# PEER feed-forward: the last 32 tokens' experts gathered for VectorE, the dense experts on 224 columns with v's weights stationary

## The chip, the cores and the metric

The kernel runs on one core of one Trainium2 chip. The metric is the device time of one execution in microseconds. TensorE (PE) multiplies matrices, VectorE (DVE) and ScalarE (ACT) work elementwise, GpSimd (POOL) does elementwise work too, and SyncE (SP) issues most of the DMAs.

## What is computed

Two blocks of 256 tokens and model width 1024: attention with a convolutional gated MLP, then a state-space and attention mixer. What the change touches is the last feed-forward, PEER, with 16384 experts, 8 heads, and 16 picks of each head, so 128 picks of each token:

```
q = (x @ w_q).reshape(bsz, seq, PEER_HEADS, 2, PEER_KEY_DIM)
s1 = einsum('bshd,hnd->bshn', q[..., 0, :], sub_k1)
s2 = einsum('bshd,hnd->bshn', q[..., 1, :], sub_k2)
v1, i1 = lax.top_k(s1, PEER_TOPK)
v2, i2 = lax.top_k(s2, PEER_TOPK)
cand_s = v1[..., :, None] + v2[..., None, :]
cand_i = i1[..., :, None] * PEER_KEYS + i2[..., None, :]
top_s, pos = lax.top_k(cand_s, PEER_TOPK)
experts = take_along_axis(cand_i, pos, axis=-1)
gates = softmax(top_s, axis=-1)
# per token: 128 experts ec, 128 gates gc
act = gelu(einsum('ced,cd->ce', u_tab[ec], xc)) * gc
out = einsum('ce,ced->cd', act, v_tab[ec])
```

The result is added to x, and a last RMS norm gives the output.

## The kernel before

**Numbers.** Activations and weights are f32 values, each split in two parts of a type that TensorE takes at a high rate: a high part, and the rest as a low part. A product is three matmuls (hi·hi, lo·hi, hi·lo; lines 154 and 157), accumulated in PSUM. Each weight tile of 128 x 1024 is loaded by SyncE (line 81), rounded by ScalarE to `whi` (line 92), and its rest `wlo` is subtracted by VectorE or, for every `share`-th tile, by GpSimd (line 94). A helper, `Weights`, does so some tiles ahead, in the order in which tiles are taken; instructions stand on each engine in the order in which the code issues them.

**Dense experts.** The kernel does not gather. It computes u for all 16384 experts and all 256 tokens, gelu, multiplies by gates that are zero where an expert was not picked, and multiplies with all of v. This takes two stages of 128 chunks, each chunk 128 experts.

*u stage.* `u_pair` (line 1695) takes two chunks into one PSUM bank: weights of u stationary, the 256 tokens of x (`hTh`, `hTl`) moving, 24 matmuls of 256 columns to a chunk, so 48 to a pair. ScalarE applies gelu into `S` (two buffers, `S0` for chunks 0 to 63, `S1` for 64 to 127). In the first 24 pairs the routing work (top-k on VectorE) is dealt out between matmuls from a list `work`, in token halves 0 and 1, and `share` is 2 in that time, 0 afterwards.

*Gates.* In the pairs of the second half of u, and in the first chunks of v, gates are made in steps: `gate_gen` builds one-hot matrices on VectorE (lines 1667, 1671, 1675), `gate_mm` multiplies them on TensorE (line 1690, 128 x 64 in bf16, 24 matmuls on average to a step), and line 1693 multiplies `S` by the result. There are 32 steps to each half of the experts.

*v stage.* For each chunk ScalarE rounds S to `ah` (line 1775), GpSimd subtracts the rest, `al` (line 1776), and 12 matmuls follow: stationary are 128 tokens of `ah` or `al`, moving are 512 columns of v's `whi` or `wlo`; four PSUM banks hold two token halves by two column halves of the output. The order is ah·whi, ah·wlo, al·whi, four each. The two buffers of `ah` and `al` let chunk c+1 be prepared while chunk c is multiplied.

*End.* The last four chunks run bank by bank, and behind each bank come the addition to x (line 1819), the sum of squares and the gain; then a reciprocal root from Newton steps (`rsqrt`, lines 170 to 177), two scalings and two output DMAs per token half. The first half's end lies beside the second half's matmuls.

Of the kernel before, what the change touches and what calls it, by code (L numbers as in the profile page):

```python
# [135 lines left out]
class Net:  # L136
# [543 lines left out]
    def arm_norm(self, gsrc, eng=None):  # L680

        g = self.load_g(gsrc, eng=eng)
        hT = self.new_T(self.hTp, "hT")
        xn, root = {}, {}
        ms = self.xnp.tile([128, 2, 2], FT, name="ms")

        def after(t, h, c):
            if h == 0:
                xn[t] = self.scratch()
            self.nc.gpsimd.tensor_tensor(xn[t][:, c], self.x[:, t, c], g[:, c], op=OP.mult)  # L690
            self.square(self.x[:, t, c], ms[:, t, h:h + 1])
# [828 lines left out]
    def peer(self, ctx, w, hT):  # L1520
# [7 lines left out]
        S0 = sp.tile([128, 64, S], FT, name="S0")  # L1528
        scr = sp.tile([128, 16384], FT, name="S1")
# [118 lines left out]
        def route5(t):  # L1648
# [46 lines left out]
        def u_pair(c, between=None):  # L1695
            ps = self.bank()
            for x in range(2):
                wt = w.next()
                if x and between:
                    between()  # L1700
                self.mm_cols(ps[:, 256 * x:256 * x + 256], wt, hT)
            if c == 64:
                late["S1"] = sp.tile([128, 64, S], FT, name="S1")
            dst = S0[:, c:c + 2] if c < 64 else late["S1"][:, c - 64:c - 62]
            w.post(lambda: nc.scalar.activation(dst, ps.rearrange("p (a b) -> p a b", a=2), AF.Gelu_apprx_tanh))

        for t in range(2):
            w.post(nc.scalar.activation, qn[:, t], self.queries[t], AF.Copy)
# [15 lines left out]
        for t in range(2):  # L1724
# [4 lines left out]
        todo = [(x, t, n) for t in range(2) for x in range(2) for n in range(2)]  # L1729
        for i in range(9):  # L1730
            if i < 8:
                work.append((lambda i=i: pick(*todo[i]), 16))
            if i:
                work.append((lambda i=i: picked(*todo[i - 1]), 16))
            if i == 4:
                work.append((lambda: route5(0), 10))
        work.append((lambda: route5(1), 10))

        def some(budget=16):
            while work and budget >= work[0][1] // 2:  # L1740
# [30 lines left out]

        def a_split(c, dst=None):
            src = S0[:, c] if c < 64 else late["S1"][:, c - 64]
            ah, al = dst or (sp.tile([128, S], FR, name=x, bufs=2) for x in ("ah", "al"))
# [4 lines left out]
        for c in range(64, 126, 2):  # L1779
            u_pair(c, lambda: gate_steps(1, 64))  # L1780
            if c == 94:
                gate_steps(1, 64)
        A = []
        u_pair(126, lambda: A.append(a_split(0)))
        w.flush()

        def v_mm(c, A, wt, th):
            self.mm3([(acc[t][h], *(x[:, 128 * t:128 * t + 128] for x in A), *(x[:, 512 * h:512 * h + 512] for x in wt),
                       c == 0, c == 127) for t, h in th], "s")

        nxt = A.pop()
        for c in range(124):
            if c == 122:

                w.parts = Room(sp.tile([128, 64 * S], FR, name="S0"))
            A = nxt
            wt = w.next()
            nxt = a_split(c + 1)
            v_mm(c, A, wt, [(t, h) for t in range(2) for h in range(2)])
            if c % 2 == (c > 30):  # L1800
                gate_steps(1, 128)

        A = [nxt] + [a_split(125 + i, [w.parts.tile([128, S]) for _ in range(2)]) for i in range(3)]
        wts = w.take(4)
        xr = self.hTp.tile([128, 2, D], FT, name="hTh")
        gb = self.hTp.tile([128, D], FT, name="hTl")
        src = a["norm_f_g"]
        nc.sync.dma_start(out=gb, in_=bass.AP(tensor=src.tensor, offset=src.offset, ap=[[0, 128], [1, D]]))
        for t in range(2):
            nc.sync.dma_start(out=xr[:, t], in_=self.xd[t])  # L1810
        j, xg = w.parts.tile([128, 512]), self.raw.tile([128, D], FT, name="raw")
        cc = [slice(512 * h, 512 * h + 512) for h in range(2)]
        for t in range(2):
            ms = self.tiny.tile([128, 2], FT, name="ms", bufs=4)
            for h in range(2):
                for i in range(4):
                    v_mm(124 + i, A[i], wts[i], [(t, h)])
                x = xr[:, t, cc[h]]
                V.tensor_tensor(x, acc[t][h], x, op=OP.add)
                nc.scalar.activation(j, x, AF.Square, scale=D ** -0.5, accum_out=ms[:, h:h + 1])  # L1820
                G.tensor_tensor(xg[:, cc[h]], x, gb[:, cc[h]], op=OP.mult)
            r = self.rstd(ms)
            for h in range(2):
                x = xr[:, t, cc[h]]
                if h:
                    V.tensor_scalar(x, xg[:, cc[h]], r, None, op0=OP.mult)
                else:
                    nc.scalar.activation(x, xg[:, cc[h]], AF.Identity, scale=r)
                (nc.sync if h else nc.scalar).dma_start(out=self.out[0, 128 * t:128 * t + 128, cc[h]], in_=x)


    def build(self):
        tc, nc, a = self.tc, self.nc, self.a
        with ExitStack() as ctx:
            ctx.enter_context(tc.manual_schedule())
            self.setup(ctx)
            with ExitStack() as b1:
# [27 lines left out]
                        hT = self.layer(l, w, hT)  # L1865
                with ExitStack() as c2:
                    hT = self.block2(c2, w, hT)
                self.xd = self.dram.tile([2, 128, D], FT, name="xd")
                for t in range(2):
                    nc.sync.dma_start(out=self.xd[t], in_=self.x[:, t])  # L1870
# [56 lines left out]
def pack(inp):  # L1927
# [65 lines left out]
    a["vs"] = rows(f("peer_v_2")[0])  # L1993
# [39 lines left out]
```

## Time and profile before

| | us |
|---|---|
| median of 3 runs | 1715.86 (1715.3 to 1719.04) |
| profiled execution, its own time | 1715.53 |
| its span | 1713.6 |
| PE busy | 1660.6 (97%) |
| PE weight loads busy | 1468.0 (86%) |
| DVE busy | 1243.8 (73%) |
| ACT busy | 850.6 (50%) |
| POOL busy | 623.3 (36%) |

The mean granted clock of TensorE in that execution is 0.992. Shares are averages over stages with different limits, so the rows below are read by stage: u takes from about 946 to 1330 us of the span (the first pairs a little before), v the rest. A matmul's record has a modelled end, so how fast matmuls follow each other is read from their starts.

### The profile page before, as it was taken

Reading aid. Unit: us, or ns where it says so; the run is one execution under the profiler, and the core shown is the slowest. Engines: PE = TensorE matmul, PEld = TensorE weight load, DVE = VectorE, ACT = ScalarE, POOL = GpSimd, SP = SyncE. Lnnn points to the kernel's source line nnn. Section 1 sums busy time; section 2 is a strip of 40 time slices with the busy share of each in tenths; the row PEclk is TensorE's granted clock in tenths of the full one; section 3 lists DMA queues with packets and bytes.
Section 4 is the critical chain, followed back from the end, with each engine's and each line's share of the span. In section 5 each row is a group of like instructions: output and inputs, shape, how many; then the busy total and the mean of one; then the engine's idle time right before and its main releaser. Section 6 shows DMA issues by size and latency. Waiting matters only on the chain.

```text
span 1713.6 us, 29782 instructions
## 1 busy us (share of the span) xinstructions
PE 1660.6 (97%) x11558; PEld 1468.0 (86%) x11558; DVE 1243.8 (73%) x2248; ACT 850.6 (50%) x1298; POOL 623.3 (36%) x534
## 2 busy tenths in 40 slices
PE   7999999999999999989989999999999999999998
PEld 6788898887889898768879999999999888888886
DVE  6775897767767776696743999677877889864445
ACT  6555554655555465543444445534344444445544
POOL 2213539332048834590020554000000343345555
PEclk9999999999999999989999999999999999999999
DMA  7444455654345567723444455654545555556564
GB/s 247 140 142 137 148 176 179 213 185 134 124 159 174 172 199 252 274 87 101 159 165 164 164 177 193 194 170 157 168 156 168 161 173 163 171 183 196 191 193 158
DMA packets 84717, 294.08 MB, mean 172 GB/s; under 512 B 10800, under 2 KB 14928, under 8 KB 83680
## 3 DMA queue, kind: packets, MB, share of 16 engines
q1 hardware_dynamic: 83184, 286.19, 51.3%
q0 software_dynamic: 960, 5.47, 0.9%
q8 instruction: 90, 1.47, 0.3%
q14 instruction: 51, 0.42, 0.1%
q10 hardware_dynamic: 432, 0.53, 0.1%
HBM read 284.42 MB, written 7.34 MB: 170 GB/s over the span
## 4 chain that ended last, share of the span: by engine, by line
PE 76%; DVE 12%; ACT 3%; POOL 3%; issue 3%; DMA 2%; ACTq 0%; DVEq 0%; POOLq 0%
PE acc L157 27%; PE side L157 17%; PE acc L154 14%; PE side L154 9%; DVE wlo L94 4%; PE side L1690 3%; DVE cv L776 1%; ACT whi L92 1%; DMA raw<-in_ws 1%; PE side L396 1%; POOL BB L967 1%; PE side L373 1%; DMA Kst<-dKst 1%; PE side L372 1%; DVE S L1508 1%
## 5 line engine op out<-in xcount | busy, mean ns | idle before, releaser
L94 DVE TENSOR_TENSOR wlo<-raw,whi 128x1024 fp32r<-128x1024 f32 x472 | 622.1, 1326 | 308.0 <-ACT whi L92 307.2
L92 ACT ACTIVATE whi<-raw 128x1024 fp32r<-128x1024 f32 x511 | 532.5, 1056 | 473.6 <-PE acc L157 233.0
L1776 POOL TENSOR_TENSOR al<-S,ah 128x256 fp32r<-128x256 f32 x125 | 171.4, 1371 | 443.3 <-ACT ah L1775 423.0
L154 PE MATMUL side<-hTh,whi 128*128 128x256 f32 x1664 | 235.5, 284 | 5.9 <-ACT whi L92 5.8
L157 PE MATMUL side<-hTh,wlo 128*128 128x256 f32 x1664 | 232.8, 282 | 1.0 <-DVE wlo L94 1.0
L157 PE MATMUL side<-hTl,whi 128*128 128x256 f32 x1664 | 233.0, 283 | 0.0
L154 PEld LDWEIGHTS side<-hTh,whi 128*128 128x128 f32 x1664 | 215.1, 191 | 10.3 <-ACT whi L92 7.2
L157 PEld LDWEIGHTS side<-hTh,wlo 128*128 128x128 f32 x1664 | 213.5, 191 | 1.4 <-DVE wlo L94 1.2
L157 PEld LDWEIGHTS side<-hTl,whi 128*128 128x128 f32 x1664 | 214.0, 191 | 0.0
L94 POOL TENSOR_TENSOR wlo<-raw,whi 128x1024 fp32r<-128x1024 f32 x39 | 98.9, 2539 | 129.0 <-ACT whi L92 126.5
L154 PE MATMUL acc<-whi,ah 128*128 128x512 f32 x496 | 134.2, 392 | 0.0
L157 PE MATMUL acc<-wlo,ah 128*128 128x512 f32 x496 | 132.7, 389 | 0.0
L157 PE MATMUL acc<-whi,al 128*128 128x512 f32 x496 | 132.7, 389 | 0.0
L154 PE MATMUL acc<-whi,hTh 128*128 128x512 f32 x384 | 123.9, 417 | 1.6 <-ACT whi L92 1.6
L157 PE MATMUL acc<-wlo,hTh 128*128 128x512 f32 x384 | 117.4, 400 | 0.7 <-DVE wlo L94 0.5
L157 PE MATMUL acc<-whi,hTl 128*128 128x512 f32 x384 | 117.2, 399 | 0.3 <-DVE hTl L220 0.3
L157 PEld LDWEIGHTS acc<-whi,al 128*128 128x128 f32 x496 | 93.1, 188 | 19.7
L157 PEld LDWEIGHTS acc<-wlo,ah 128*128 128x128 f32 x496 | 93.1, 188 | 19.6
L784 POOL TENSOR_TENSOR th<-th,cv 128x256 f32<-128x256 f32 x44 | 58.3, 1327 | 138.2 <-DVE th L783 109.4
L154 PEld LDWEIGHTS acc<-whi,ah 128*128 128x128 f32 x496 | 91.9, 188 | 18.1
L776 DVE SCALAR_TENSOR_TENSOR cv<-side,cw,cv 128x254 f32<-128x254 f32 (+1 forms) x176 | 72.6, 474 | 29.1 <-ACT cv L773 29.1
L157 PEld LDWEIGHTS acc<-wlo,hTh 128*128 128x128 f32 x384 | 72.9, 190 | 19.5 <-DVE wlo L94 1.8
(459 smaller groups left out, 2434.0 us busy)
## 6 DMA issues: line engine op xcount, KB each, us to landing
raw<-in_ws SPq DMA_DIRECT2D x259, 512.0 KB, 4.2
raw<-in_us SPq DMA_DIRECT2D x128, 512.0 KB, 3.8
raw<-in_vs SPq DMA_DIRECT2D x128, 512.0 KB, 4.2
dBst<-Bst SPq DMA_DIRECT2D x1, 2048.0 KB, 7.3
dCT<-CT SPq DMA_DIRECT2D x2, 1024.0 KB, 8.1
tg<-dBst POOLq DMA_DIRECT2D x1, 2048.0 KB, 11.4
gb<-in_g_ffn SPq DMA_DIRECT2D x2, 512.0 KB, 5.2
s5bc<-in_s5bc SPq DMA_DIRECT2D x2, 512.0 KB, 5.4
```

The lines of the kernel that those rows point to most:

```text
L92: self.nc.scalar.activation(hi, t, AF.Copy)
L94: eng.tensor_tensor(lo, t, hi.bitcast(FT), op=OP.subtract)
L154: mm(ps, sh, mh, start=first, stop=False)
L157: mm(ps, sl if side == "s" else sh, ml if side == "m" else mh, start=False, stop=last and side == late)
L372: nc.tensor.matmul(ps[:, 0:128], u["q"][:, 0:128], u["k"][:, 0:128], start=True, stop=True)
L373: nc.tensor.matmul(ps[:, 128:384], u["q"][:, 128:256], u["k"][:, 0:256], start=True, stop=True)
L396: nc.tensor.transpose(ps[:, 128 * i:128 * i + 128], u["p"][:, 128 * i:128 * i + 128], self.ident)
L776: nc.vector.scalar_tensor_tensor(o[which][:, n:], p[which][:, :S - n], cw[which][:, 2 - n:3 - n], o[which][:, n:], op0=OP.mult, op1=OP.add)
L784: nc.gpsimd.tensor_tensor(th, th, o[1], op=OP.mult)
L967: G.tensor_tensor(o[i][p, :, g2], t[0][p], t[1][p], op=op)
L1690: nc.tensor.matmul(o, e2[:, n], e1[:, n, x], start=x == 0, stop=x == 2)
L1776: G.tensor_tensor(al, src, ah.bitcast(FT), op=OP.subtract)
```

## The change

Tokens 224 to 255 leave the dense computation. All dense tiles have N = 224 token columns: u's moving operand, S, and gates (28 steps per half instead of 32). In v the operands change places: `whi` or `wlo` slices of 128 output columns are stationary and the 224 tokens of `ah` or `al` move, so v takes 24 matmuls to a chunk, the output is transposed, and the end turns it back with 16 TensorE transposes.

The 32 tokens' 4096 picks stand on 128 partitions by 32 (four groups of partitions, each with 32 of a token's picks). `pairs` makes their expert numbers `eid`. `dot_step(n)`, one for each u pair from the 29th on, has GpSimd issue an indirect DMA of 128 rows of u (a new input `un`, three buffers `rows`), and VectorE multiply the rows fetched two steps earlier with the tokens' x (`xs`) and sum along the row. `sum_step(n)`, one for each second v chunk from 52 on, does the same with rows of v, scaled and accumulated; two f32 matmuls with a 0/1 matrix `picks` add the four groups, and the result is added to x. `xs` comes from 32 normalized rows spilled to DRAM and read four times. Routing runs on token half 1 first. GpSimd takes every sixth weight split in the second half of u. The final loads of x and the gain move from SyncE behind v to ScalarE's queue at chunk 8 of v. The end handles output columns in three pieces, and takes one root for both halves.

```
+        N, GR = S - NS, 128 // NS
+        for g in range(GR):
+            nc.sync.dma_start(out=xs[NS * g:NS * g + NS], in_=self.hd)
+        hTd = tuple(x[:, :, 0:N] for x in hT)
...
+        def fetch(table, n):
+            if n < NS:
+                r = sp.tile([128, D], FT, name="rows", bufs=3)
+                G.indirect_dma_start(out=r, out_offset=None, in_=table,
+                                     in_offset=bass.IndirectOffsetOnAxis(ap=eid[:, n:n + 1], axis=0))
+                fetched.append(r)
+        def dot_step(n):
+            fetch(a["un"], n)
+            if 2 <= n < NS + 2:
+                r = fetched.popleft()
+                V.scalar_tensor_tensor(r, r, 1.0, xs, op0=OP.mult, op1=OP.mult, accum_out=dots[:, n - 2:n - 1])
...
+        def sum_step(n):
+            fetch(vn, n)
+            if 2 <= n < NS + 2:
+                r, y, m = fetched.popleft(), late["sum"], dots[:, n - 2:n - 1]
...
+                    V.scalar_tensor_tensor(y, r, m, y, op0=OP.mult, op1=OP.add)
+            if n == NS + 1:
+                for h in range(2):
+                    ps = self.bank()
+                    nc.tensor.matmul(ps, late["picks"], late["sum"][:, 512 * h:512 * h + 512], start=True, stop=True)
...
-                self.mm_cols(ps[:, 256 * x:256 * x + 256], wt, hT)
+                self.mm_cols(ps[:, 256 * x:256 * x + N], wt, hTd)
...
-        for t in range(2):
+        for t in (1, 0):
             for i in range(0, 16, 2):
                 work += zip(route1(t, i), (12, 8))
...
+        for c in range(64, 128, 2):
+            w.share = 6
...
+                u_pair(c, lambda: gate_steps(1, NQ))
+            dot_step((c - U0) // 2)
...
-            self.mm3([(acc[t][h], *(x[:, 128 * t:128 * t + 128] for x in A), *(x[:, 512 * h:512 * h + 512] for x in wt),
-                       c == 0, c == 127) for t, h in th], "s")
+            self.mm3([(acc[k // 2][:, 256 * (k % 2):256 * (k % 2) + N], *(x[:, 128 * k:128 * k + 128] for x in wt), *A[i],
+                       c == 0 and k % 2 == 0, last and k % 2 == 1 and i == len(A) - 1) for k in ks for i, wt in enumerate(wts)], "s")
...
+            if c >= V0 and c % 2 == 0:
+                sum_step((c - V0) // 2)
...
+                nc.tensor.transpose(late["turn"][t][tok[t], 128 * (k - k0):128 * (k - k0) + 128],
+                                    oT[k // 4][:, k % 4, 128 * t:128 * t + tok[t].stop], self.ident)
...
+        r = self.rsqrt(v, 2)
```

TensorE, one chunk of v. Before (stationary and moving operand behind the arrow in the program's order: moving first):

```order
L154 MATMUL acc<-whi,ah 128x512 x4
L157 MATMUL acc<-wlo,ah 128x512 x4
L157 MATMUL acc<-whi,al 128x512 x4
```

and now:

```order
L156 MATMUL acc<-ah,whi 128x224 x8
L159 MATMUL acc<-al,whi 128x224 x8
L159 MATMUL acc<-ah,wlo 128x224 x8
```

`al` is now asked for behind eight matmuls, where it was behind eight of 512 columns; the whole chunk has 24 instead of 12.

GpSimd, the v stage: `al` is the low part of S, `rows` the gathered rows. Before:

```order
L1776 TENSOR_TENSOR al<-S_9259,ah 128x256 x64
L1776 TENSOR_TENSOR al<-S_12131,ah 128x256 x61
L1776 TENSOR_TENSOR S_18723<-S_12131,S_18723 128x256 x3
```

and now, a piece from the middle:

```order
L1837 TENSOR_TENSOR al<-S_9261,ah 128x224 x2
L1686 DMA rows<-in_vs,eid 128x1024
L1837 TENSOR_TENSOR al<-S_9261,ah 128x224 x2
L1686 DMA rows<-in_vs,eid 128x1024
L1837 TENSOR_TENSOR al<-S_9261,ah 128x224 x2
L1686 DMA rows<-in_vs,eid 128x1024
L1837 TENSOR_TENSOR al<-S_12161,ah 128x224 x2
```

An indirect DMA stands in front of every second `al`.

VectorE, the second half of u: `wlo` is a weight split, `e` and `eq` are the one-hot matrices, `S` times `side` the gates, `rows` times `xs` a dot. Before:

```order
L94 TENSOR_TENSOR wlo<-raw,whi 128x1024
L1693 TENSOR_TENSOR S_9259<-S_9259,side 128x64x8 x2
L94 TENSOR_TENSOR wlo<-raw,whi 128x1024
L1667 TENSOR_TENSOR e_14554<-itb,ixT 128x1024
L1671 TENSOR_TENSOR eq<-itb,ixT 128x512
L1675 TENSOR_TENSOR e_14558<-eq,gT 128x1536
L94 TENSOR_TENSOR wlo<-raw,whi 128x1024 x2
```

and now:

```order
L96 TENSOR_TENSOR wlo<-raw,whi 128x1024
L1750 TENSOR_TENSOR S_9261<-S_9261,side 128x64x8 x2
L1724 TENSOR_TENSOR e_13757<-itb,ixT 128x1024
L1728 TENSOR_TENSOR eq<-itb,ixT 128x512
L1732 TENSOR_TENSOR e_13761<-eq,gT 128x1536
L1695 SCALAR_TENSOR_TENSOR rows,dots<-rows,xs 128x1024
L96 TENSOR_TENSOR wlo<-raw,whi 128x1024 x2
```

Each pair has one instruction more, `rows` times `xs`, and some splits are missing, since GpSimd has them.

## Rows read from the trace of the kernel before

**Rows 1.** Windows: us, busy by engine (instructions), clock, DMA share, GB/s.
```profile
core 0: us, PE busy (x) PEld busy (x) DVE busy (x) ACT busy (x) POOL busy (x), PEclk, DMA share, GB/s
946.00:1084.20 138.20, 137.22 (x1144) 137.02 (x1143) 134.84 (x416) 69.11 (x82) 67.48 (x25) 1.00 0.56 182
1084.20:1130.30 46.10, 46.10 (x422) 46.06 (x421) 28.11 (x30) 21.13 (x27) 0.00 (x0) 1.00 0.56 181
1140.00:1326.00 186.00, 186.00 (x2087) 185.36 (x2086) 142.42 (x176) 73.97 (x86) 0.00 (x0) 1.00 0.51 162
...
1510.00:1690.00 180.00, 180.00 (x837) 149.09 (x836) 86.53 (x74) 91.06 (x133) 96.46 (x66) 1.00 0.60 190
690.00:710.00 20.00, 18.72 (x90) 14.60 (x90) 12.83 (x33) 10.82 (x16) 7.08 (x2) 1.00 0.98 392
```

**Rows 2.** Timeline, PE around a gate step in u: start us, us, line, shapes, xcount.
```profile
1166.04 1.57 PE L1690 MATMUL side<-e,e 128*128 128x64 bf16 x48
...
1168.48 1.12 PE L157 MATMUL side<-hTl,whi 128*128 128x256 f32 x8
...
1169.44 1.12 PE L157 MATMUL side<-hTh,wlo 128*128 128x256 f32 x8
```

**Rows 3.** Timeline, one chunk of v, PE, ACT and POOL.
```profile
1600.55 1.47 POOL L1776 TENSOR_TENSOR al<-S,ah 128x256 fp32r<-128x256 f32 x1 [1.25 <-ACT ah L1775]
...
1601.63 1.07 PE L154 MATMUL acc<-whi,ah 128*128 128x512 f32 x4
...
1602.80 0.40 ACT L1775 ACTIVATE ah<-S 128x256 fp32r<-128x256 f32 x1
...
1603.44 1.07 PE L157 MATMUL acc<-whi,al 128*128 128x512 f32 x4
...
1604.35 1.07 PE L154 MATMUL acc<-whi,ah 128*128 128x512 f32 x4
```

**Rows 4.** Timeline, PE runs of other shapes, from three places.
```profile
693.56 1.08 PE L154 MATMUL acc<-hTh,whi 128*40 128x256 f32 x8
...
694.47 1.07 PE L157 MATMUL acc<-hTl,whi 128*40 128x256 f32 x8
...
712.41 1.89 PE L1246 MATMUL side<-u,tg 128*128 128x64 f32 x16
...
907.38 1.06 PE L1595 MATMUL side<-S 128*128 128x128 f32 x8
```

**Rows 5.** DVE groups by form, 1140 to 1326 us; the last row 946 to 1084.
```profile
L94 DVE TENSOR_TENSOR wlo<-raw,whi 128x1024 fp32r<-128x1024 f32 x57 | 69.7, 1223 | 43.4 <-ACT whi L92 43.4
L1675 DVE TENSOR_TENSOR e<-eq,gT 128x1536 bf16<-128x1536 bf16 x29 | 27.8, 958 | 1.0
L1667 DVE TENSOR_TENSOR e<-itb,ixT 128x1024 bf16<-128x1024 bf16 x30 | 20.5, 684 | 0.3 <-PE side L1690 0.3
L1693 DVE TENSOR_TENSOR S<-S,side 128x512 f32<-128x512 f32 x30 | 19.2, 680 | 0.0
L1671 DVE TENSOR_TENSOR eq<-itb,ixT 128x512 bf16<-128x512 bf16 x30 | 12.5, 418 | 0.0
...
L94 DVE TENSOR_TENSOR wlo<-raw,whi 128x1024 fp32r<-128x1024 f32 x24 | 36.5, 1523 | 1.1 <-ACT whi L92 0.8
```

**Rows 6.** Timeline, POOL: a DMA issue, and a weight split.
```profile
891.90 0.60 POOL L1532 DMA_DIRECT2D it<-in_iota  x1 [9.41 <-ACT S L106]
...
946.98 2.40 POOL L94 TENSOR_TENSOR wlo<-raw,whi 128x1024 fp32r<-128x1024 f32 x1 [3.35 <-ACT whi L92]
```

**Rows 7.** Timeline, the tail.
```profile
1705.34 0.69 DVE L1819 TENSOR_TENSOR hTh<-acc,hTh 128x512 f32<-128x512 f32 x1 [0.57 <-PE acc L157]
...
1707.69 0.21 DVE L177 TENSOR_SCALAR rs_y<-rs_t,rs_y 128x1 f32<-128x1 f32 x1
...
1709.12 0.72 ACT L1828 ACTIVATE hTh<-raw,rs_y 128x512 f32<-128x512 f32 x1 [2.27 <-DVE rs_y L177]
```

**Rows 8.** The page's DMA issues: count, KB each, us to landing.
```profile
raw<-in_us SPq DMA_DIRECT2D x128, 512.0 KB, 3.8
```

More of the change, by code (lines that the diff above doesn't have):

```diff
@@ L35 @@
 NEG = -1e30
+NS = 32
 EPS = 1e-6
@@ L1660, in route5, with pairs @@
                     g = grest
+        def pairs():
+            s = slice(128 - NS, 128)
+            for g in range(GR):
+                p, c = slice(NS * g, NS * g + NS), slice(NS * g, NS * g + NS)
+                V.scalar_tensor_tensor(eidf[p], sel[s, 0, 1, c], 128.0, sel[s, 1, 1, c], op0=OP.mult, op1=OP.add)
+                V.tensor_copy(gs[p], sel[s, 2, 1, c])
+            V.tensor_copy(eid, eidf)
+        fetched = deque()
+        def fetch(table, n):
[10 more added lines that the diff above has]
+            if n == NS + 1:
+                nc.scalar.activation(dots, dots, AF.Gelu_apprx_tanh)
+                V.tensor_tensor(dots, dots, gs, op=OP.mult)
+                late["sum"] = sp.tile([128, D], FT, name="xs")
+        def sum_step(n):
+            fetch(vn, n)
+            if 2 <= n < NS + 2:
+                r, y, m = fetched.popleft(), late["sum"], dots[:, n - 2:n - 1]
+                if n == 2:
+                    V.tensor_scalar(y, r, m, None, op0=OP.mult)
+                else:
+                    V.scalar_tensor_tensor(y, r, m, y, op0=OP.mult, op1=OP.add)
+            if n == NS + 1:
+                for h in range(2):
+                    ps = self.bank()
+                    nc.tensor.matmul(ps, late["picks"], late["sum"][:, 512 * h:512 * h + 512], start=True, stop=True)
+                    x = late["xr"][128 - NS:128, 1, 512 * h:512 * h + 512]
+                    w.post(V.tensor_tensor, x, ps[128 - NS:128], x, op=OP.add)
+        vn = a["vs"].rearrange("a b c -> (a b) c")
         def gate_gen(hf, q):
@@ L1723, in peer @@
             work.append((lambda t=t: route2(t), 2))
-        for t in range(2):
+        for t in (1, 0):
             for h in range(0, 8, 2):
@@ L1728, in peer @@
             work += zip(gates(t), (3, 6))
-        todo = [(x, t, n) for t in range(2) for x in range(2) for n in range(2)]
+        todo = [(x, t, n) for t in (1, 0) for x in range(2) for n in range(2)]
         for i in range(9):
@@ L1735, in peer @@
             if i == 4:
-                work.append((lambda: route5(0), 10))
-        work.append((lambda: route5(1), 10))
+                work.append((lambda: route5(1), 10))
+                work.append((pairs, 8))
+        work.append((lambda: route5(0), 10))
         def some(budget=16):
@@ L1777, in a_split, with v_mm @@
             return ah, al
[L1779 to L1787, printed above, removed]
-            self.mm3([(acc[t][h], *(x[:, 128 * t:128 * t + 128] for x in A), *(x[:, 512 * h:512 * h + 512] for x in wt),
-                       c == 0, c == 127) for t, h in th], "s")
+        for c in range(64, 128, 2):
+            w.share = 6
+            if c == 126:
+                w.share = 0
+                A = []
+                u_pair(c, lambda: (gate_steps(1, NQ), A.append(a_split(0))))
+                w.flush()
+            else:
+                u_pair(c, lambda: gate_steps(1, NQ))
+            dot_step((c - U0) // 2)
+        acc = acc[0] + acc[1]
+        def v_mm(c, A, wts, ks, last=False):
+            self.mm3([(acc[k // 2][:, 256 * (k % 2):256 * (k % 2) + N], *(x[:, 128 * k:128 * k + 128] for x in wt), *A[i],
+                       c == 0 and k % 2 == 0, last and k % 2 == 1 and i == len(A) - 1) for k in ks for i, wt in enumerate(wts)], "s")
         nxt = A.pop()
@@ L1798, in peer @@
             nxt = a_split(c + 1)
-            v_mm(c, A, wt, [(t, h) for t in range(2) for h in range(2)])
+            v_mm(c, [A], [wt], range(8))
             if c % 2 == (c > 30):
-                gate_steps(1, 128)
-        A = [nxt] + [a_split(125 + i, [w.parts.tile([128, S]) for _ in range(2)]) for i in range(3)]
-        wts = w.take(4)
[L1805 to L1808, printed above, removed]
@@ L1809, in peer @@
-        for t in range(2):
[L1810 to L1814, printed above, removed]
-            for h in range(2):
[L1816 to L1824, printed above, removed]
+                gate_steps(1, 2 * NQ)
@@ new lines, in peer @@
+            if c == 8:
+                xr = late["xr"] = self.hTp.tile([128, 2, D], FT, name="hTh")
+                gb = self.hTp.tile([128, D], FT, name="hTl")
+                src = a["norm_f_g"]
+                nc.scalar.dma_start(out=gb, in_=bass.AP(tensor=src.tensor, offset=src.offset, ap=[[0, 128], [1, D]]))
+                for t in range(2):
+                    nc.scalar.dma_start(out=xr[:, t], in_=self.xd[t])
+                late["picks"] = sp.tile([128, 128], FT, name="it")
+                nc.scalar.dma_start(out=late["picks"], in_=a["sums"])
@@ new lines, in peer @@
+            if c >= V0 and c % 2 == 0:
+                sum_step((c - V0) // 2)
+        A = [nxt] + [a_split(125 + i, [w.parts.tile([128, N]) for _ in range(2)]) for i in range(3)]
+        wts = w.take(4)
+        oT = [sp.tile([128, D], FT, name="rows", bufs=3)[:, 0:4 * N].rearrange("p (k n) -> p k n", k=4) for _ in range(2)]
+        j = w.parts.tile([128, 512])
+        xg = [self.raw.tile([128, D], FT, name="raw") for _ in range(2)]
+        ms = self.tiny.tile([128, 2, 3], FT, name="ms3")
@@ new lines, in peer, with turn @@
+        pieces = [(0, 4), (4, 6), (6, 8)]
+        tok = [slice(0, 128), slice(0, N - 128)]
+        def turn(k):
+            i = max(i for i in range(3) if pieces[i][0] <= k)
+            k0, k1 = pieces[i]
+            if k == k0:
+                late["turn"] = [self.bank() for _ in range(2)]
+            for t in range(2):
+                nc.tensor.transpose(late["turn"][t][tok[t], 128 * (k - k0):128 * (k - k0) + 128],
+                                    oT[k // 4][:, k % 4, 128 * t:128 * t + tok[t].stop], self.ident)
+            if k < k1 - 1:
+                return
+            c = slice(128 * k0, 128 * k1)
+            for t in range(2):
+                x = xr[:, t, c]
+                V.tensor_tensor(x[tok[t]], late["turn"][t][tok[t], 0:128 * (k1 - k0)], x[tok[t]], op=OP.add)
+                nc.scalar.activation(j[:, 0:128 * (k1 - k0)], x, AF.Square, scale=D ** -0.5, accum_out=ms[:, t, i:i + 1])
+                G.tensor_tensor(xg[t][:, c], x, gb[:, c], op=OP.mult)
@@ new lines, in peer @@
+        for b in range(4):
+            for k in (2 * b, 2 * b + 1):
+                v_mm(124, A, wts, [k], True)
+            for i in range(2):
+                src, dst = acc[b][:, 256 * i:256 * i + N], oT[b // 2][:, 2 * (b % 2) + i]
+                if i:
+                    nc.scalar.activation(dst, src, AF.Copy)
+                else:
+                    V.tensor_copy(dst, src)
+            for k in (2 * b - 2, 2 * b - 1) if b else ():
+                turn(k)
+        turn(6)
+        turn(7)
```

44 lines of the change are left out of this document (29 added, 15 removed).

## The prediction, made before the changed kernel had run

> **What bounds the kernel now.** I read the windows view of the expert stages first [rows 1]. Between 946 and 1690 us TensorE is busy for 137.22 of 138.20, 46.10 of 46.10, 186.00 of 186.00 and 180.00 of 180.00 us in the four stretches that matter, at a granted clock of 1.00 (its 2.4 GHz level): every gap between matmuls counts, and work on another engine only where that engine becomes later than TensorE. One is close: VectorE, 134.84 of 138.20 us in the first stretch. Then the timeline of one gate step among the u matmuls [rows 2], one chunk of v [rows 3], places where TensorE runs other shapes [rows 4], VectorE's groups [rows 5], GpSimd's instructions [rows 6] and the tail [rows 7].
>
> **Spacing now.** Eight 256-column matmuls start .96 us before the next eight [rows 2]: 120 ns each, so a u pair of 48 takes 5.76 us. A v chunk is 12 of 512 columns in 2.72 us (1601.63 to 1604.35) [rows 3], 226.7 ns each. Forty-eight gate matmuls and the eight behind them take 2.44 us [rows 2]; less .96 the gates cost 1.48, so .74 per step (24 matmuls).
>
> **The new spacing X, the term that decides.** All dense matmuls get 224 columns; no row has that. From 256 to 512 columns a column costs (226.7 - 120)/256 = .417 ns; down to 224 this gives 120 - 13.3 = 106.7. That is one end. The other is 120, no gain at all. Between them lies what a weight load allows. An f32 matmul is recorded as two passes, each with its own load of 128 weight columns; eight passes over 128 columns are busy for 1.06 us [rows 4], and with the last one's modelled duration (I estimate .275, from 1.12 less seven times .120 in rows 2) taken off, seven intervals of .112 remain. Sixteen passes over 64 columns take 1.89 [rows 4], (1.89 - .275)/15 = .108: half the columns and nearly the same spacing, so it isn't the columns that set it, and the load is what they share. With only 40 weight columns in the load, 256 columns take (694.47 - 693.56)/8 = 114 ns [rows 4] against 120. I take X = 112, since the load stands in every new matmul and these rows lie nearest in columns from below; both ends are kept.
>
> **u stage (24 matmuls per chunk, as before).** First 24 pairs: TensorE alone needs 24 x 48 x .112 = 129.0, VectorE 134.84 [rows 1]; VectorE's routing is the same work in another order, so 138.2 becomes 134.8: -3.4. Next 8 pairs: VectorE 28.1 of 46.1, so 43.0: -3.1. Second half before: 32 x 5.76 + 32 x .74 = 208.0. After: 32 x 48 x .112 = 172.0, and 28 steps (56 groups of four tokens for 64) at .74 = 20.7, together 192.7. VectorE there: of 64 weight splits every sixth goes to GpSimd, 53.3 x 1.223 = 65.2; 28 x (.958 + .684 + .680 + .418 = 2.74) = 76.7 [rows 5]; 30 dot instructions of 128x1024 with two f32 inputs. No row has such an instruction; the plain subtraction of that size is 1.22 [rows 5], I take 1.30: 39.0. Sum 180.9. GpSimd's 10.7 splits also hold VectorE up: in the first stretch 24 VectorE splits average 1523 instead of 1223 ns beside 25 instructions of GpSimd, nearly all of them splits [rows 1, 5]; 24 x .30 = 7.2, spread over some 24 splits of GpSimd's .30 for each; the other end is their whole 2.40 alone [rows 6]. I take .30, the same instruction beside VectorE: 3.2. VectorE's 184.1 stays under TensorE; for holdups between two engines so nearly equal I add 1.0, what TensorE lost in the first stretch (138.20 - 137.22). So 193.7: -14.3. u together -20.8.
>
> **v stage.** 128 x 12 x .2267 = 348.2 becomes 128 x 24 x .112 = 344.1: -4.1. Turning the operands round doubles the matmuls, so v gains nearly nothing though 32 columns are gone. Four gate steps fewer: -3.0. Twelve transposes between the last matmuls x .112: +1.3; two f32 matmuls of 512 columns for the gathered sum, four passes x .227 x 2 = +1.8. VectorE gets 32 sums x 1.30 = 42, most after the gates, where it has 180 - 86.5 us free [rows 1]. Together -4.0.
>
> **What is queued behind the gathers.** Each gather is issued by GpSimd between `al` subtractions, one per two v chunks. `al` of a chunk ends at 1602.02 (1600.55 + 1.47), .39 after its chunk began (1601.63), and is wanted 1.81 after [rows 3]. In the new order whi·al stands second, after 8 x .112 = .90. If a gather starts as an `al` ends, its issue time G and the next `al` (1.47 x 224/256 = 1.29) must be done by 2.69 + .90: .39 + G + 1.29 <= 3.59, so G <= 1.9. Rows have a direct GpSimd issue of .60 [rows 6]; an indirect one isn't shown, and I bound it by .60 and by GpSimd's longest nearby instruction, 2.40 [rows 6], whose excess of .5 in each of 32 gathers costs 16. I take under 1.9: 0, covered by TensorE's own matmuls. The rows themselves are wanted two steps later (2 x 5.4 us), where 0.5 MB loads land in 3.8 [rows 8]. Traffic grows by .5 MB per 6 us, 87 GB/s on 181; the trace has moved 392 at a share of .98 [rows 1], so weights still come in time. In u the splits on GpSimd stand behind gathers too, but are asked for two tiles ahead.
>
> **Start and tail.** The spill of 32 rows and the four reloads stand on SyncE ahead of the whole peer stage, the first dot behind 30 of its u pairs: 0, up to 3 if weight loads behind them are late. The final row and gain loads move to ScalarE's queue at chunk 8: 0. The tail grows: after the last accumulation both halves must be copied out (.4, as `ah` [rows 3]), transposed and added (.5), and one Newton root for two columns has six more small VectorE instructions, .21 each [rows 7], less .3 from a shorter last addition; a second ScalarE scaling of .72 [rows 7] follows the first. .4 + .5 + 1.3 - .3 + .72 = +2.6; bounds 0 and 5.
>
> **Sum.** -20.8 - 4.0 + 2.6 = -22.2 against the profiled execution's own 1715.5 (span 1713.6), .3 under the median shown: 1693.
>
> **Rivals.**
> (a) X stays 120: something paces a matmul whatever its columns up to 256. For: 114 and 120 at equal columns. Against: 112 at 128 and 64. u: only the 4 gate steps, -3.0; v: 3072 x .120 = 368.6, +20.4 - 3.0 + 3.1; tail +2.6. Sum +20: 1736.
> (b) VectorE and GpSimd exclude each other wholly in u's second half. VectorE then has 180.9 + 10.7 x 2.40 = 206.6, and with 34 gather issues of .60, 227.0. Instead of -14.3 this gives -1.4 to +19: 1706 to 1727. For: GpSimd's splits there beside a full VectorE were never run; against: the .30.
> (c) The slower side, by one mechanism: the gather's issue in v, pinned behind VectorE, delays `al`. If it has to sit out one split (1.23) and one sum (1.30), G = .60 + 2.53 = 3.1, 1.2 over the 1.9, and 32 x 1.2 = 39 gives 1732. From G = 1.9 + 22/32 = 2.6 it is slower than before. For: `al` itself takes 1.47 beside a VectorE split for a quarter of its width [rows 3]. Against: while VectorE is free there half the time, a short issue need not wait.
> The Trainium skill, "SBUF — State Buffer", section "SBUF: two separate sides", speaks for (c): a GpSimd-issued DMA of some 620 ns alone took some 3100 beside a VectorE copy, since descriptors wait for a shared port. No run here shows it yet; by its 3.1 the time would be that of (c).
> (d) X is column bound, 106.7. u: -3.4, -5.1, and the second half is held by VectorE at 185.1, -22.9; v 3072 x .1067 = 327.8, -20.4 + .1; tail +2.6: 1666, or 1677 where each GpSimd split costs VectorE 1.36. For: the slope from 256 to 512. Against: 112 at fewer columns.
> The Trainium skill, "TensorE: Matmul & The Clock Gate", section "Back-to-back issue gap", would go further: columns/2.4 + 2.5, 95.8 ns at 224. The trace disagrees at 256, 120 against its 109.
> (e) The split-precision type has no full rate under 256 columns. No such matmul has fewer in this kernel, so no row excludes it. Like f32 (two passes of .112 per 128 columns, [rows 4]) a matmul would take .224 x 224/128 = .39: u 3072 x (.39 - .12) = 829 more, v 3072 x .39 - 348 = 850 more, about 3390.
>
> **How the numbers follow.** Forecast .48, own range 1686 to 1706; (a) .12; (b) .13; (c) .13; (d) .09; (e) .05. A measurement of this kernel tells .2%, 3.4 us, from no change. Faster: .48 + .09 + .05 of (b) + .02 of (c) = .64. Same: .05 of (b), .02 of (c) = .07. Slower: .12 + .03 + .09 + .05 = .29. The range goes from 1672, inside (d), to 1737, with (a); outside lie (e), half of (d) and the far part of (c).
>
> **What would show it.** In the new trace: eight 224-column u matmuls starting .90 us apart (107 ns: .85, 120: .96); a v chunk of 2.69 without gates; the u stage's second half near 194 us with TensorE's idle time put down to nothing, not to `wlo`; `al` never the releaser of TensorE; gather issues under 1.9 us. I am wrong if TensorE waits for `wlo` or `al` over 5 us in all, or if its spacing is outside 109 to 115.

## The result, and the profile after

The changed kernel takes 1691.88 us (median of 4, 1691.01 to 1696.48) where the kernel before takes 1716.49 beside it: ratio .986, 95% interval .9838 to .9882, 24.6 us faster. The forecast was 1693, in a range of 1672 to 1737. The profiled execution of the changed kernel is the longest of the four, 1696.48 with a span of 1694.3; where that matters, it is said.

The windows view of the kernel before, cut at the same places of the program as the next one: u's first 24 pairs, its next 8, its other 32, and v from the start of its first matmul to the end of its last (columns as in [rows 1]):

```profile
937.90:1077.76 139.86, 138.88 (x1158) 138.68 (x1157) 136.50 (x444) 71.30 (x84) 69.89 (x26) 1.00 0.54 177
1077.76:1124.16 46.40, 46.40 (x389) 46.40 (x388) 29.48 (x31) 22.55 (x29) 0.00 (x0) 1.00 0.58 184
1124.16:1332.16 208.00, 208.00 (x2306) 207.31 (x2305) 156.79 (x192) 83.28 (x97) 1.47 (x1) 1.00 0.52 163
1332.16:1705.30 373.14, 373.14 (x2306) 309.09 (x2304) 255.32 (x261) 175.38 (x260) 177.05 (x130) 1.00 0.56 178
```

The changed kernel, the same four:

```profile
943.30:1078.50 135.20, 131.74 (x1159) 130.97 (x1158) 131.88 (x452) 69.84 (x85) 70.09 (x26) 0.99 0.56 180
1078.50:1121.68 43.18, 43.18 (x389) 43.18 (x388) 32.75 (x35) 21.88 (x29) 6.18 (x5) 1.00 0.74 247
1121.68:1314.10 192.42, 192.42 (x2210) 192.04 (x2209) 183.73 (x229) 81.63 (x98) 71.26 (x39) 1.00 0.75 254
1314.10:1683.10 369.00, 367.69 (x3760) 365.67 (x3759) 279.35 (x271) 172.77 (x261) 189.26 (x161) 1.00 0.68 226
```

| stretch (all in us) | forecast | profiles |
|---|---|---|
| before u (937.90 to 943.30) | 0 (0 to 3) | +5.4 |
| u, first 24 pairs | -3.4 | -4.7 |
| u, next 8 pairs | -3.1 | -3.2 |
| u, other 32 pairs | -14.3 | -15.6 |
| v | -4.0 | -4.1 |
| tail (8.30 to 11.20) | +2.6 | +2.9 |
| outside the span (1.93 to 2.18) | 0 | +.25 |
| sum | -22.2 | -19.05 = 1696.48 - 1715.53 |

The first line belongs mostly to this execution: in the profiles of the ten kernels below, all with the same start, u begins at 937.9 to 941.0 us, middle 939.5, so +1.6 rather than +5.4; in this one TensorE's granted clock was .83 between 770 and 780 us, where the kernel before had 1.00. The first 24 pairs also lost 1.7 us in this execution: at a wait of 2.06 us for `wlo` the clock fell to its 1.2 GHz level (granted .64 on average from 1000.5 to 1003.9 us), and sixteen matmuls took 3.48 us (1001.52 to 1005.00) instead of 1.79. With +1.6, and without this 1.7, the sum is -24.5, near the medians' difference. TensorE's timeline there:

```profile
1001.52 2.05 PE L159 MATMUL side<-hTh,wlo 128*128 128x224 f32 x8 [2.06 <-DVE wlo L96]
1003.37 1.79 PE L156 MATMUL side<-hTh,whi 128*128 128x224 f32 x8
1005.00 1.05 PE L159 MATMUL side<-hTl,whi 128*128 128x224 f32 x8
```

TensorE among the u matmuls and in one chunk of v of the changed kernel, with GpSimd and VectorE there (timeline; start us, us):

```profile
986.27 1.05 PE L156 MATMUL side<-hTh,whi 128*128 128x224 f32 x8
987.17 1.06 PE L159 MATMUL side<-hTl,whi 128*128 128x224 f32 x8
...
1559.41 1.06 ACT L94 ACTIVATE whi<-raw 128x1024 fp32r<-128x1024 f32 x1 [1.33 <-PE acc L159]
1560.11 1.06 PE L156 MATMUL acc<-ah,whi 128*128 128x224 f32 x8
1560.38 0.38 ACT L1836 ACTIVATE ah<-S 128x224 fp32r<-128x224 f32 x1
1560.84 1.42 POOL L1837 TENSOR_TENSOR al<-S,ah 128x224 fp32r<-128x224 f32 x1 [1.19 <-ACT ah L1836]
1561.65 1.70 DVE L1709 SCALAR_TENSOR_TENSOR xs<-rows,dots,xs 128x1024 f32<-128x1024 f32 x1
1562.42 1.76 POOL L1686 DMA_INDIRECT rows<-in_vs,eid  x1 [0.16 <-issue]
1562.79 1.06 PE L156 MATMUL acc<-ah,whi 128*128 128x224 f32 x8
1564.19 0.81 POOL L1837 TENSOR_TENSOR al<-S,ah 128x224 fp32r<-128x224 f32 x1
...
1565.47 1.06 PE L156 MATMUL acc<-ah,whi 128*128 128x224 f32 x8
```

Eight matmuls take .90 us in u, so 112 ns each, and a chunk of v takes 2.68 (1562.79 to 1565.47) where it took 2.72 [rows 3]. The gather occupies GpSimd for 1.76 us and the `al` behind it ends at 1565.00, .47 before its chunk begins; in the kernel before it ended .39 after [rows 3]. No wait of TensorE for `wlo` or `al` is listed for u's second half, and in v only .9 us for tiles of the last chunks and .5 at the sum's two matmuls.

### The profile page after: what moved, and what is told of

The parts are those of the page before. It is cut to its first block, busy times and chain, and to the rows that moved or that the text cites. A ratio compares the mean times of both kernels' runs of the same rounds, so it can differ in the third digit from the quotient of the medians.

```text
span 1694.3 us, 32761 instructions
## 1 busy us (share of the span) xinstructions
PE 1631.9 (96%) x12922; PEld 1500.4 (89%) x12922; DVE 1294.9 (76%) x2315; ACT 847.1 (50%) x1307; POOL 715.8 (42%) x610
## 4 chain that ended last, share of the span: by engine, by line
PE 71%; DVE 14%; POOL 5%; ACT 5%; issue 3%; DMA 2%; ACTq 0%; POOLq 0%; SPq 0%; DVEq 0%
PE acc L159 27%; PE side L159 14%; PE acc L156 14%; PE side L156 7%; DVE wlo L96 4%; PE side L1747 2%; ACT whi L94 2%; DVE cv L778 2%; POOL th L786 1%; DMA raw<-in_ws 1%; PE side L398 1%; DMA Kst<-dKst 1%; PE side L375 1%; POOL bt L965 1%; PE side L374 1%
## 5 line engine op out<-in xcount | busy, mean ns | idle before, releaser
L156 PE MATMUL side<-hTh,whi 128*128 128x224 f32 (+1 forms) x1664 | 228.5, 280 | 6.1 <-ACT whi L94 6.1
L159 PE MATMUL side<-hTh,wlo 128*128 128x224 f32 (+1 forms) x1664 | 226.0, 278 | 2.7 <-DVE wlo L96 2.3
L159 PE MATMUL side<-hTl,whi 128*128 128x224 f32 (+1 forms) x1664 | 224.3, 277 | 0.0
L1837 POOL TENSOR_TENSOR al<-S,ah 128x224 fp32r<-128x224 f32 x125 | 131.7, 1054 | 173.5 <-ACT ah L1836 172.9
L156 PE MATMUL acc<-ah,whi 128*128 128x224 f32 x992 | 132.5, 276 | 0.0
L159 PE MATMUL acc<-ah,wlo 128*128 128x224 f32 x992 | 131.0, 274 | 0.0
L159 PE MATMUL acc<-al,whi 128*128 128x224 f32 x992 | 131.0, 274 | 0.0
L156 PEld LDWEIGHTS acc<-ah,whi 128*128 128x128 f32 x992 | 120.8, 192 | 0.5 <-issue 0.5
L159 PEld LDWEIGHTS acc<-al,whi 128*128 128x128 f32 x992 | 120.8, 192 | 0.0
L159 PEld LDWEIGHTS acc<-ah,wlo 128*128 128x128 f32 x992 | 120.7, 192 | 0.0
L159 PEld LDWEIGHTS acc<-wlo,hTh 128*128 128x128 f32 x384 | 73.2, 191 | 19.2 <-DVE wlo L96 1.3
```

The costliest lines, as they stand in the source:

```text
L156: mm(ps, sh, mh, start=first, stop=False)
L159: mm(ps, sl if side == "s" else sh, ml if side == "m" else mh, start=False, stop=last and side == late)
```

## The experiments

Edits are against the changed kernel.

**v turned back.** The end is that of the kernel before, on 128 and 96 rows.

```
-            self.mm3([(acc[k // 2][:, 256 * (k % 2):256 * (k % 2) + N], *(x[:, 128 * k:128 * k + 128] for x in wt), *A[i],
...
+            self.mm3([(acc[t][h][tok[t]], *(x[:, 128 * t:128 * t + tok[t].stop] for x in A), *(x[:, 512 * h:512 * h + 512] for x in wt),
...
```

> The changed kernel with v turned back: 128 or 96 of the 224 tokens stationary, 512 columns of v moving, 12 matmuls to a chunk, the end of before without transposes; all else as changed. Theory (a weight load paces 224-column matmuls at about 112 ns, so v gained only .04 us per chunk by turning): chunks of 2.72 instead of 2.68 us, 124 x .04 = +5.0, no 16 transposes -1.8, the shorter end -1.2: +2 us against the changed kernel, 1694. Rival (turning v is what makes the 32 tokens less pay in v): 96 stationary columns cost as much as 128, so all of 32/256 of v's 344 us comes back, +40, 1732.

1700.88 us (median of 5, ratio .9911, .9898 to .9925): 9 slower than the changed kernel, clear of its interval, so more than the +2 of my theory and far from +40. TensorE's timeline in that kernel:

```profile
1599.96 1.11 PE L159 MATMUL acc<-wlo,ah 128*128 128x512 f32 x4
...
1602.76 1.09 PE L159 MATMUL acc<-wlo,ah 128*128 128x512 f32 x4
```

A chunk takes 2.80 here, 2.78 on average, so a 512-column matmul 232 ns and not the 226.7 of [rows 3]: 124 chunks x .10 = +12, less a cheaper end. Two more runs looked for the reason.

```
+            self.mm3([(acc[t][h], *(x[:, 96 * t:96 * t + 128] for x in A), ...
```

> The kernel with v turned back (the first run here), with 128 stationary tokens in both halves, the second half taking tokens 96 to 223; the output of the second half is not placed rightly. v's 512-column matmuls followed at 231 to 232 ns in that run against 226.7 in the kernel before. Theory (96 stationary tokens are the reason): 226.7 again, chunks 2.72. Rival 1 (the reason lies elsewhere, in the narrower tiles or the traffic): 231 stays, chunks 2.78.

2.78 to 2.79 again (1703.11): not the 96 stationary tokens.

```
-            ah, al = dst or (sp.tile([128, N], FR, name=x, bufs=2) for x in ("ah", "al"))
+            ah, al = dst or (sp.tile([128, S], FR, name=x, bufs=2)[:, 0:N] for x in ("ah", "al"))
```

> The kernel with v turned back (the first run), with ah and al tiles of 256 columns, of which 224 are used, so that they lie in memory as in the kernel before. Theory (the place of the stationary tiles makes 512-column matmuls follow at 231 instead of 226.7): 226.7 and chunks of 2.72. Rival (not the tiles, but what else goes on, gathers and traffic): 231 and 2.78.

2.78 again (1700.37): not the tiles' width. The chunks ahead of the first gather have it as well, so not the gathers. Nor is 232 peculiar to this build: the 512-column matmuls of the layers ahead of PEER follow at 232 to 235 ns (medians) in the kernel before as well, and v of the kernel before, at 227, is the exception. Why it is stays open. Turning v was worth 9 us in this kernel all the same, most of it by that unexplained difference.

**Without the gathers.** `dot_step`, `sum_step` and `pairs` are not called.

> The changed kernel without the gathers, the dots, the sums and their two matmuls; the PEER output of the last 32 tokens is left out. Theory (gathers lie wholly beside TensorE): only the 2.4 us of the two matmuls and their wait go: 1689 to 1690. Rival (gathers cost through the port, the DMA traffic or GpSimd's queue): 10 us or more faster, below 1682.

1688.35 (median of 5, ratio .9841, .9828 to .9855), 3.5 faster than the changed kernel by the medians, with intervals that overlap, and far from the rival's 10. Its windows for u's second half and v, same cuts:

```profile
1115.29:1307.65 192.36, 192.36 (x2210) 192.04 (x2209) 152.47 (x166) 81.24 (x97) 25.89 (x11) 1.00 0.54 176
1307.65:1674.15 366.50, 365.69 (x3756) 364.82 (x3755) 229.68 (x237) 172.50 (x261) 152.43 (x129) 1.00 0.56 182
```

u's second half is 192.36 against 192.42, though VectorE has 31 us and the DMAs 78 GB/s less: its gathers and 31 dots cost nothing there. v is 2.5 shorter (366.50 against 369.00): the two f32 matmuls for the sum (their chunks take 4.73 and 3.07 instead of 2.68, 2.44 together).

**More issue time on GpSimd in v.** One or two small gathers, read by nobody, behind each gather (one of 128 columns, or two of 64; the second is shown):

```
+            for _ in range(2 if n < NS else 0):
+                e = sp.tile([128, 64], FT, name="rows2", bufs=4)
+                G.indirect_dma_start(out=e, out_offset=None, in_=a["iota"].rearrange("p (a b) -> (p a) b", b=64),
+                                     in_offset=bass.IndirectOffsetOnAxis(ap=eid2[:, n:n + 1], axis=0))
```

> The changed kernel with a second indirect gather (128 rows of a 128-wide table, read by nobody) behind each gather in the v stage, so that GpSimd is held about 3.4 us instead of 1.76 in front of every second al. In the changed kernel's trace al ends .46 us before its chunk starts and is wanted .90 after, 1.36 to spare. Theory (al late beyond that margin holds TensorE): 1.7 - 1.36 = .3 us late, or up to .95 where al then falls beside a weight split and takes 1.42 instead of .81: 32 x .3 to .95 = +10 to +30, with al as TensorE's releaser. Rival (the issue time of a gather doesn't matter since the queue catches up): within 2 us of the changed kernel.

With one more: 1697.32 (median of 4, ratio .9888, .9873 to .9903), 5.4 slower than the changed kernel, between the two theories; the two intervals just overlap (.9882 and .9873), so the profile says more. A small gather took only .95 us plus .30 in front of it, so GpSimd was held 3.0; `al` ended up to .88 us after its chunk's start, just ahead of the .90, and TensorE lost .04 to .14 in some chunks, 1.7 in v. Another .7 lies in u's next 8 pairs (43.93 instead of 43.20), just behind the five VectorE copies that make the small gathers' row numbers. The rest of the 5.4 isn't placed.

> The changed kernel with two extra small gathers behind each gather of v, each held GpSimd some 1.25 us (.95 and .30 of issue) in the run with one. With one, al ended up to .87 us after its chunk's start and is wanted at .90. Theory: 1.25 us later again, so TensorE waits 1.2 us for al in each of 32 double chunks, +35 to +40 against the changed kernel, about 1730, slower than the kernel before: the slower rival of the prediction, with its point where the issue takes 3.0 instead of 1.9 us. Rival (al overtakes elsewhere and nothing waits): within 5 us of 1695.

With two (a single run): 1749.04, slower than the kernel before; v took 423.20 us, 54 more than in the changed kernel. Its timeline, then its window of v and its list of TensorE's waits there (total us, times, longest):

```profile
1600.79 0.96 POOL L1691 DMA_INDIRECT rows<-in_vs,eid  x1 [0.16 <-issue]
...
1601.36 1.23 DVE L96 TENSOR_TENSOR wlo<-raw,whi 128x1024 fp32r<-128x1024 f32 x1 [1.25 <-ACT whi L94]
...
1602.06 1.35 POOL L1711 DMA_INDIRECT rows<-in_iota,eid  x1 [0.31 <-issue]
...
1603.71 0.94 POOL L1711 DMA_INDIRECT rows<-in_iota,eid  x1 [0.30 <-issue]
...
1604.67 3.27 POOL L1846 TENSOR_TENSOR al<-S,ah 128x224 fp32r<-128x224 f32 x2
...
1606.38 1.15 PE L159 MATMUL acc<-al,whi 128*128 128x224 f32 x8 [1.68 <-POOL al L1846]
```

```profile
1312.00:1735.20 423.20, 385.26 (x3760) 378.86 (x3759) 290.47 (x271) 173.19 (x261) 259.87 (x225) 0.97 0.63 202
PE acc L159 <- POOL al L1846: 36.6, 24, 1.7
```

This is the slower rival (c), as a mechanism: an `al` behind too long an issue holds TensorE, 1.5 us on average and at most 1.7. These waits, 24 listed for 32 gathers, are 36.6 of the 54 us; each is longer than the 1.2 expected, since a late `al` falls beside VectorE's split and sum and takes 1.64 instead of .81. The other 17.6 us are TensorE busy longer (385.26 against 367.69) with the same number of matmuls: the granted clock over v is .97 where the changed kernel has 1.00, and behind one of the waits, between 1486.5 and 1490 us, it is .57. The clock makes some 13 of the 17.6, an estimate from .03 x 423; the expectation had only the waits. The point where TensorE begins to wait is 3.0 us, not 1.9.

**A ladder of widths.** 22 of the 24 matmuls of a u chunk on other widths in the first half of u, and v's chunks 60 to 123 on fewer columns; the columns left out are missing from the sums.

> The changed kernel with other moving widths: u chunks by eights with 256, 256, ... stepwise 256 (24 chunks... pairs 1 to 6), 240 (6 pairs), 208 (6), 192 (6), 160 (4), 128 (4) columns in 22 of 24 matmuls, then 224 in the rest; in v 224 to chunk 59, then 192, 160 and 128 columns for 20, 20 and 24 chunks. Columns left out are left out of the sums. Theory (a floor by the weight load, and 13 ns over the columns above it): median spacing 120 ns at 256, 113.3 at 240, 112 at 224 and the same 112 at 208, 192, 160 and 128. Rival 1 (spacing follows the columns): 100 at 208, 93 at 192, 80 at 160, 67 at 128. Rival 2 (the split type loses its rate at some width): several times 112 from there on.

TensorE's timeline at 256, 240 and 128 columns in u, and at 128 in v:

```profile
947.02 1.12 PE L1764 MATMUL side<-hTh,whi 128*128 128x256 f32 x8
947.98 1.12 PE L1766 MATMUL side<-hTl,whi 128*128 128x256 f32 x8
...
978.32 1.06 PE L1764 MATMUL side<-hTh,whi 128*128 128x240 f32 x8
979.21 1.06 PE L1766 MATMUL side<-hTl,whi 128*128 128x240 f32 x8
...
1109.17 1.06 PE L1766 MATMUL side<-hTl,whi 128*128 128x128 f32 x8
1110.06 1.10 PE L1769 MATMUL side<-hTh,wlo 128*128 128x128 f32 x8
...
1635.05 1.06 PE L156 MATMUL acc<-ah,whi 128*128 128x128 f32 x8
1635.94 1.06 PE L159 MATMUL acc<-al,whi 128*128 128x128 f32 x8
```

The starts lie .96 us apart at 256 columns and .89 to .90 at 240 and at 128; medians of single spacings are 120 at 256, 112 at 240, and 111 to 112 at 224, 208, 192, 160 and 128. Nothing under 240 columns gets faster, nothing gets slower: 1693.63 (a single run) for the whole kernel, like the changed one although a good part of its columns is gone. Rival (d) and rival (e) of the prediction are both out.

**No sixths on GpSimd.** `w.share = 0` in u's second half.

> The changed kernel with all weight splits of u's second half on VectorE (none of the sixths on GpSimd). Theory (splits cost VectorE about 1.22 each and little when GpSimd has them; TensorE is held only where VectorE goes past it): VectorE's 183.7 us of 192.4 become 183.7 + 10 x 1.22 less the collisions with GpSimd's ten, at most 22 us less, so 174 to 196 against TensorE's 192.4: 0 to +4 us, 1692 to 1696. Rival (VectorE and GpSimd exclude each other wholly, so the sixths cost more than they relieve): faster by 2 or more, below 1690.

1690.63 (median of 5, ratio .985, .9836 to .9865), the changed kernel's time. Its window of u's second half, then VectorE's groups there, the changed kernel's first, this one's behind:

```profile
1116.12:1308.50 192.38, 192.38 (x2211) 192.06 (x2210) 179.30 (x239) 81.40 (x98) 47.69 (x29) 1.00 0.72 255
```

```profile
L96 DVE TENSOR_TENSOR wlo<-raw,whi 128x1024 fp32r<-128x1024 f32 x54 | 65.2, 1220 | 6.0 <-ACT whi L94 6.0
L1695 DVE SCALAR_TENSOR_TENSOR rows<-rows,xs 128x1024 f32<-128x1024 f32 x31 | 37.8, 1219 | 0.0
L1724 DVE TENSOR_TENSOR e<-itb,ixT 128x1024 bf16<-128x1024 bf16 x28 | 34.6, 1237 | 0.4 <-PE side L1747 0.4
```

```profile
L96 DVE TENSOR_TENSOR wlo<-raw,whi 128x1024 fp32r<-128x1024 f32 x64 | 77.2, 1223 | 10.8 <-ACT whi L94 10.8
...
L1724 DVE TENSOR_TENSOR e<-itb,ixT 128x1024 bf16<-128x1024 bf16 x28 | 19.2, 684 | 0.0
```

VectorE has ten splits more and is busy 4.4 us less (179.30 against 183.73). The ten on GpSimd took 12.0 us off its splits and put 15.4 on the one-hot compares: nine of the 28 were held, by 1.7 each (the tenth split met a small product of the dots, 2.0 instead of .2). How, the changed kernel's timeline shows:

```profile
1156.09 2.40 POOL L96 TENSOR_TENSOR wlo<-raw,whi 128x1024 fp32r<-128x1024 f32 x1 [5.13 <-ACT whi L94]
1156.61 2.44 DVE L1724 TENSOR_TENSOR e<-itb,ixT 128x1024 bf16<-128x1024 bf16 x1
```

A compare of .68 that starts inside a GpSimd split ends .56 us behind it (1159.05 against 1158.49), and so do the other eight, wherever in the split they start: it stood until GpSimd was done. The gate products, which read one of their inputs from PSUM, keep their .68 inside the same splits. The time is the same because TensorE bounds this half in both.

**More splits on GpSimd in the first 24 pairs**, `i % 5 in (0, 2, 4)` in place of every second.

> The changed kernel with 3 of 5 instead of 1 of 2 weight splits on GpSimd in u's first 24 pairs. In its trace TensorE needs 24 x 5.36 = 128.7 there and took 135.2 (133.6 to 133.9 in the profiles of the runs before this one). Theory (VectorE's routing and splits bound that stretch): some 5 splits less on VectorE, 5 x 1.22 less what GpSimd's holds it up: -2 to -5 us, 1687 to 1690. Rival (the waits there come from single long instructions in the routing and from GpSimd's own lateness, 2.4 us a split against 2.68 per tile): within 2 us, or slower.

1693.48 (median of 5, ratio .9872, .9851 to .9893): not faster, the rival. The stretch takes 135.7; one wait of 1.8 is now for a GpSimd split.

**Two conversions to ScalarE**, and no sixths.

```
-            V.tensor_copy(i16b[:, t], i16[:, t])
+            nc.scalar.activation(i16b[:, t], i16[:, t], AF.Copy)
...
```

> The changed kernel with no sixths on GpSimd in u's second half (as in the fifth run) and with two conversions of integer tables to bf16 in the routing moved from VectorE (3.6 and .9 us in the first stretch) to ScalarE, which is half idle there. Theory (VectorE's routing bounds the first 24 pairs, where TensorE loses 5 us): about 4.5 us less on VectorE, -2 to -4 us against 1691: 1687 to 1689. Rival (the waits come from how the work is dealt between matmuls, not from its sum): within 1 us.

1691.09 (median of 4, ratio .9852, .9836 to .9869): the rival again. VectorE is busy 125.23 us in the first 24 pairs instead of 130.28 in the run without sixths, but they take 132.97 instead of 133.54:

```profile
937.85:1070.82 132.97, 130.84 (x1158) 129.62 (x1157) 125.23 (x448) 71.38 (x88) 71.69 (x26) 1.00 0.56 183
```

So 4 us over TensorE's 128.7 (24 pairs of 5.36) remain there with VectorE no longer full. How the routing lies between the matmuls is what is left to suspect; that wasn't tried. No version that computes the whole result beats the changed kernel by more than its spread.

## Why the prediction was right

**The spacing X = 112.** Right: 112 at 224 columns, and the ladder shows the floor from 128 to 240. That the load of weights makes the floor is argued and not shown, since every matmul of the ladder loads 128 weight columns. With the same load in bf16 the gate matmuls follow at 31 ns (1.48 us for 48 [rows 2]), so it isn't the floor of every type. And in the kernel before 16 f32 passes that load only 32 weight columns take 1.94 us, which by the prediction's own working, (1.94 - .275)/15, is .111 as well. So its f32 rows do not single out the load, and what makes the floor stays open:

```profile
595.98 1.94 PE L1048 MATMUL side<-CT,B 128*32 128x128 f32 x16
```

The low end I kept (106.7, the slope of the columns) and the high end (120) are both off by 5 ns or more. By the formula of the Trainium skill weighed there ("TensorE: Matmul & The Clock Gate", "Back-to-back issue gap"), which the page gives for a single isolated matmul, it would have been 95.8; the trace has 112.

**u.** The second half came out at 192.42, TensorE's own 192.7 without the 1.0 for holdups. The first 24 pairs were near by luck: the forecast of -3.4 took VectorE's sum of 134.84 for the bound, and they take 133 to 134 us in most profiles (135.2 here, by the fallen clock). With 5 us less on VectorE, two conversions being on ScalarE, they are only .6 shorter (132.97 for 133.54), so its sum is not what holds them.

**VectorE's 184.1 in u's second half was right by two errors.** It was busy 183.73. The step "I take .30" for a GpSimd split's cost failed: nine of the ten cost 1.7 each. The .30 was an average that I misread: of the 24 VectorE splits behind it [rows 5], 19 took 1.20 to 1.31, and the other five, 1.57 to 4.19, make up all of the 7.2. Most of GpSimd's splits stood beside short routing instructions; a VectorE split that did start inside one was held to its end, in the kernel before already:

```profile
1005.83 2.41 POOL L94 TENSOR_TENSOR wlo<-raw,whi 128x1024 fp32r<-128x1024 f32 x1 [3.43 <-ACT whi L92]
...
1007.08 2.24 DVE L94 TENSOR_TENSOR wlo<-raw,whi 128x1024 fp32r<-128x1024 f32 x1
```

The other error offsets this one: rows' durations overlap by about .05 each, which the sum counted twice: in the run without sixths six groups add up to 190.6 us (77.2 + 37.8 + 19.2, and 26.8, 17.9 and 11.7 for the rest) in 179.30 busy. The dots took 1.22, not 1.30. Near the edge between two engines such a sum could have gone either way; here 8.7 us were left to TensorE's 192.42, so rival (b) had its mechanism and not its price. The Trainium skill ("SBUF — State Buffer", "Who interferes with whom") calls the contention of VectorE and GpSimd at their shared port an exclusive lock. The compare of 2.44 and the split of 2.24 agree, and it was the rule to use.

**v and tail.** v came out at -4.1 for -4.0, from four terms that are each off: spacing gave -5.1 (128 x .04) for -4.1, fewer gate steps -3.8 for -3.0 (by the chunks' starts), the two f32 matmuls cost 2.44 for 1.8, and the last four chunks 2.3 for the 1.3 of the transposes, with .9 of waits for their tiles. The tail is +2.9 for +2.6. That the errors in v cancel to .1 is luck.

**The gathers.** "Under 1.9" held narrowly (1.76), and the margin behind it was mis-sized: with one more the point was 3.0. The inequality took `al`'s place in the chunk from before. But whi·al now stands second, so `whi` comes free a third of a chunk earlier, and ScalarE's rounding of the next tile begins .70 us ahead of the chunk (1559.41 against 1560.11) instead of .20 behind it, and with it `ah` and `al` come .9 earlier:

```profile
1601.83 1.06 ACT L92 ACTIVATE whi<-raw 128x1024 fp32r<-128x1024 f32 x1 [1.35 <-PE acc L157]
```

That is the row of the kernel before, whose chunk began at 1601.63 [rows 3]. I had priced the earlier need and not the earlier supply. Rival (c)'s 3.1 us for an issue beside VectorE didn't appear: the 64 gathers take .94 to 1.76, the longest beside its splits and sums. The some 3100 ns that the Trainium skill ("SBUF — State Buffer", "SBUF: two separate sides") gives for an issue beside a VectorE copy are thus not what this trace shows beside other instructions.

**Start.** The forecast of 0 was nearly right: +1.6 by the middle of the other profiles.

## What to carry to other kernels

When a matmul gets fewer columns, look for rows with few columns, a full load of weights and operands of the same size: their spacing is the floor (112 ns here for four bytes, 31 for bf16), and taking away columns under it gains nothing. When a part of the order is changed, work out anew when buffers come free, not only when they are wanted. And price GpSimd's help by the VectorE instruction that will stand beside it, not by the one it replaces, and not by an average over instructions most of which met nothing.

## What was unexpected of the hardware

The floor holds without a step from 240 to 128 columns. An indirect gather of 128 rows of 4 KB keeps GpSimd for .94 to 1.76 us (middle 1.68 in u and 1.76 in v, mostly beside VectorE's splits and sums), and lands after 5.3 to 8.9 us (middle 6.2). Of two VectorE instructions of 128x1024 with two f32 inputs, the dot with a constant takes 1219 ns and the sum with a scalar from memory 1695:

```profile
L1709 DVE SCALAR_TENSOR_TENSOR xs<-rows,dots,xs x31: 1693/1695/1697, 1492.0 to 1652.8; 128x1024 f32<-128x1024 f32 x31
```

And 512-column matmuls of one and the same shape follow at 227 ns in v of the kernel before and at 232 in its layers and in every other build of v, which no run here explains.
